# Batched matmul of transposed inputs: b loaded for two batches at once, eight rows per partition, one transpose for both

## The chip, the cores and the metric

One core of a Trainium2 chip. The metric is the device time of one execution in microseconds (us); lower is better. Engines are named as the profile names them: PE is TensorE's matmul, PEld its weight load, DVE is VectorE, ACT is ScalarE, SP is SyncE, whose queue (SPq) issues every DMA here. "16 engines" are the core's DMA engines.

## The reference

```python
batch, m, k, n = 16, 512, 512, 512
a: (batch, k, m) float32,  b: (batch, n, k) float32

def reference(a, b):
    return np.matmul(a.transpose(0, 2, 1), b.transpose(0, 2, 1)).astype(np.float32)
```

Per batch 1 MB of a and 1 MB of b come in and 1 MB of result goes out: 50.33 MB in all. b has its contraction axis k last, so it must be transposed on the chip.

## The kernel before

Each batch is one round of a loop: load b and a, cast a to bf16 on ACT, transpose b on PE in f32 into PSUM, cast the transposed b to bf16 on DVE (the "cast" of this document), multiply, evict the result on ACT and DVE in turn, store the result of six batches earlier.

```python
a_v = a.rearrange("b (ki ko) m -> b ki ko m", ko=KO)      # 4 consecutive rows (8 KB) per partition
b_v = b.rearrange("b (no ni) k -> b ni no k", ni=P)       # rows 128 apart: pieces of 2 KB
out_v = out.rearrange("b (mi mo) n -> b mi mo n", mo=MO)  # 8 KB per partition
# ... pools: a 3, b 3, a in bf16 4, bt 3, o 8 buffers; psum_t 4, psum_o 4 banks
LAG = 6
for i in range(B):
    b_sb = b_pool.tile([P, NO, K], f32)
    nc.sync.dma_start(b_sb, b_v[i])
    # ... load a, cast it to a_bf on ACT
    for rk in range(KO):
        bt_ps = psum_t.tile([P, N], f32)
        for no in range(NO):
            nc.tensor.transpose(bt_ps[:, no * P:(no + 1) * P], b_sr[:, no, rk, :], identity)
        nc.vector.tensor_copy(bt_sb[:, rk, :], bt_ps)     # the cast: contiguous in, contiguous out
    # ... 16 matmuls into o_ps, evictions to o_sb by ACT and DVE in turn
    if i >= LAG:
        emit_out_dma(i - LAG)
```

## Time and profile before

| | before |
|---|---|
| time, median of the first 3 runs | 129.39 us (129.38 to 129.58) |
| span in the profile | 127.8 us |
| DMA queue, share of 16 engines' span | 97.5% |
| one cast of transposed b (DVE) | 683 ns |

From the page of the kernel before: the busy line, then rows of the view that cuts the span into 40 equal slices. A digit is the busy share of that slice in tenths; PEclk is the clock granted to TensorE; DMA is the mean of the 16 engines.

```profile
PE 92.5 (72%) x504; PEld 60.6 (47%) x512; DVE 61.5 (48%) x96; ACT 54.8 (43%) x97; POOL 0.7 (1%) x6
...
PE   0099999999999995768767796877779777670000
DVE  0053668586774865463544727355472635640000
PEclk9999999999999999999999999999999999998555
DMA  3999999999999999999999999999999999999980
...
q1 hardware_dynamic: 13056, 50.33, 97.5%
```

The DMA row is 9 nearly from end to end while PE and DVE have room: the kernel is bound by its transfers. The groups of instructions say what one instruction costs; the columns are busy us, mean ns of one, then the idle time just before them and who ended it.

```profile
L80 PE MATMUL o_ps<-bt_sb,a_bf 128*128 128x512 bf16 x248 | 59.0, 385 | 9.1 <-ACT a_bf L60 8.7
...
L73 DVE CAST bt_sb<-bt_ps 128x512 bf16<-128x512 f32 x64 | 40.0, 683 | 14.7 <-PE bt_ps L68 14.7
L68 PE MATMUL bt_ps<-identity,b_sb 128*128 128x128 f32 x256 | 35.7, 295 | 12.8 <-DMA b_sb<-in_b_dram 12.8
```

### The profile page before, as it was taken

What the parts mean: (1) busy time and instruction counts of PE and PEld (TensorE: products, weight loads), DVE (VectorE), ACT (ScalarE), POOL (GpSimd) and SP (SyncE); (2) the same over time, 40 slices, a digit from 0 to 9 for tenths busy, and PEclk for the clock granted to TensorE, in tenths of its full rate; (3) what the DMA queues carried; (4) which work ended last, traced back from release to release, by engine and by line L of the source; (5) the groups of instructions that cost most, each with busy time, mean ns of one, the idle gap of its engine ahead of it and who ended that gap; (6) DMA issues with size and microseconds to landing.
All of it is one profiled execution on the core that took longest, in us unless ns stands there. A gap on an engine that the chain in (4) does not pass through costs nothing.

```text
span 127.8 us, 1405 instructions
## 1 busy us (share of the span) xinstructions
PE 92.5 (72%) x504; PEld 60.6 (47%) x512; DVE 61.5 (48%) x96; ACT 54.8 (43%) x97; POOL 0.7 (1%) x6
## 2 busy tenths in 40 slices
PE   0099999999999995768767796877779777670000
PEld 0094858678586763364634536353364634430000
DVE  0053668586774865463544727355472635640000
ACT  4026747646674635407163460816337072540000
POOL 2000000000000000000000000000000000000000
PEclk9999999999999999999999999999999999998555
DMA  3999999999999999999999999999999999999980
GB/s 90 402 370 422 406 399 420 382 409 398 404 417 415 417 419 394 416 410 429 420 410 423 406 436 405 416 426 413 427 402 431 412 424 418 426 428 428 426 346 36
DMA packets 13063, 50.42 MB, mean 394 GB/s; under 512 B 768, under 2 KB 768, under 8 KB 8960
## 3 DMA queue, kind: packets, MB, share of 16 engines
q1 hardware_dynamic: 13056, 50.33, 97.5%
q8 instruction: 4, 0.07, 0.2%
q14 instruction: 3, 0.02, 0.0%
HBM read 33.55 MB, written 16.78 MB: 394 GB/s over the span
## 4 chain that ended last, share of the span: by engine, by line
DMA 50%; PE 34%; SPq 3%; ACT 1%; issue 1%; DVE 1%; ACTq 0%
DMA a_sb<-in_a_dram 32%; PE o_ps L80 22%; DMA out_dram<-o_sb 13%; PE bt_ps L68 12%; DMA b_sb<-in_b_dram 4%; SPq L56 3%; ACT a_bf L60 1%; DVE o_sb L90 1%; ACT o_sb L88 0%; ACTq L60 0%; SPq L50 0%
## 5 line engine op out<-in xcount | busy, mean ns | idle before, releaser
L80 PE MATMUL o_ps<-bt_sb,a_bf 128*128 128x512 bf16 x248 | 59.0, 385 | 9.1 <-ACT a_bf L60 8.7
L60 ACT CAST a_bf<-a_sb 128x512 bf16<-128x512 f32 x64 | 34.9, 615 | 39.6 <-DMA a_sb<-in_a_dram 39.5
L73 DVE CAST bt_sb<-bt_ps 128x512 bf16<-128x512 f32 x64 | 40.0, 683 | 14.7 <-PE bt_ps L68 14.7
L68 PE MATMUL bt_ps<-identity,b_sb 128*128 128x128 f32 x256 | 35.7, 295 | 12.8 <-DMA b_sb<-in_b_dram 12.8
L80 PEld LDWEIGHTS <-a_bf 128*128 128x128 bf16 x256 | 27.3, 115 | 35.8 <-ACT a_bf L60 17.7
L68 PEld LDWEIGHTS bt_ps<-identity,b_sb 128*128 128x128 f32 x256 | 33.9, 211 | 17.5 <-PE o_ps L80 8.5
L90 DVE COPY o_sb<-o_ps 128x512 f32<-128x512 f32 x32 | 22.1, 692 | 38.9 <-PE o_ps L80 21.9
L88 ACT COPY o_sb<-o_ps 128x512 f32<-128x512 f32 x32 | 18.8, 586 | 19.0 <-PE o_ps L80 18.9
L60 ACT ACT_TABLE_LOAD x1 | 1.3, 1283 | 0.7 <-PEq L111 0.7
masks.py:199 POOL TENSOR_SCALAR_AFFINE_SELECT identity<-identity 128x128 f32<-128x128 f32 x1 | 0.3, 292 | 0.1
masks.py:197 POOL MEMSET identity<- 128x128 f32 x1 | 0.2, 204 | 0.3 <-POOLq L111 0.3
L111 POOL MEMSET const-bfloat16-1.0<- 128x1 bf16 x1 | 0.1, 101 | 0.0
L111 POOL MEMSET const-uint8-127<- 128x1 uint8 x1 | 0.1, 101 | 0.0
L111 POOL MEMSET const-float32-0.0<- 128x1 f32 x1 | 0.1, 98 | 0.2 <-issue 0.2
L111 POOL MEMSET const-float32-1.0<- 128x1 f32 x1 | 0.1, 98 | 0.0
## 6 DMA issues: line engine op xcount, KB each, us to landing
b_sb<-in_b_dram SPq DMA_DIRECT2D x16, 1024.0 KB, 15.4
a_sb<-in_a_dram SPq DMA_DIRECT2D x16, 1024.0 KB, 17.3
out_dram<-o_sb SPq DMA_DIRECT2D x16, 1024.0 KB, 17.4
```

The costliest lines, as they stand in the source:

```text
L56: nc.sync.dma_start(a_sb, a_v[i])
L60: nc.scalar.copy(a_bf[:, rk, :], a_sb[:, rk, :])
L68: nc.tensor.transpose(bt_ps[:, no * P:(no + 1) * P], b_sr[:, no, rk, :], identity,)
L73: nc.vector.tensor_copy(bt_sb[:, rk, :], bt_ps)
L80: nc.tensor.matmul(o_ps, a_br[:, rk, rm, :], bt_sb[:, rk, :], start=(rk == 0), stop=(rk == KO - 1),)
L88: nc.scalar.copy(o_sb[:, rm, :], o_ps)
L90: nc.vector.tensor_copy(o_sb[:, rm, :], o_ps)
L111: nc = _bacc.Bacc("TRN2", target_bir_lowering=False, num_devices=1)
```

## The change

The intent: b arrives in pieces of 2 KB, the other two tensors in pieces of 8 KB. If each partition takes eight consecutive rows of b, its piece is 16 KB. 64 partitions then hold one batch of 512 rows, so one load of 2 MB covers two batches, and each 128x128 transpose covers both. A transposed block holds every eighth row of each batch, so the cast has to put its columns back in order: it writes bf16 elements eight apart. The stores follow three batches behind rather than six, with buffers moved between pools.

```diff
-    b_v = b.rearrange("b (no ni) k -> b ni no k", ni=P)
+    b_v = b.rearrange("(h g) (ni r) k -> h (g ni) r k", g=G, r=R)      # G = 2, NI = 64, R = 8
...
-    a_pool bufs=3, ac_pool bufs=4, bt_pool bufs=3, o_pool bufs=8; LAG = 6
+    a_pool bufs=5, ac_pool bufs=3, bt_pool bufs=2, o_pool bufs=6; LAG = 3
...
+        if i % G == 0:
+            b_sr = b_sb.rearrange("p r (pk rk) -> p r rk pk", rk=KO)
+            bt_pair = bt_pool.tile([P, G, KO, N], cdt)
+            bt_w = bt_pair.rearrange("p g rk (ni r) -> p rk r g ni", r=R)
+            H = R // 2
+            for rk in range(KO):
+                for h in range(2):
+                    bt_ps = psum_t.tile([P, H, G, NI], f32)
+                    for r in range(H):
+                        nc.tensor.transpose(bt_ps[:, r, :, :], b_sr[:, h * H + r, rk, :], identity)
+                    nc.vector.tensor_copy(bt_w[:, rk, h * H:(h + 1) * H, :, :], bt_ps)
+        bt_sb = bt_pair[:, i % G, :, :]
```

(The pool lines are abridged.) In the cast, the last `tensor_copy`, the innermost loop of the output is `ni`, and neighbouring `ni` lie eight bf16 elements, 16 bytes, apart.

## The prediction

> **What bounds it now.** The DMA engines, not TensorE. In the 40-slice view the mean busy share of the 16 DMA engines is 9 tenths or more from the second slice to the last but two, while PE falls to 6-8 tenths in mid-run. The queue view gives the one hardware queue 97.5% of 16 engines' span (127.8 us, so 124.6 us); about 3.2 us of the span is not DMA. The waits view agrees: ScalarE waits 39.5 us for loads of a, PE's transposes 12.8 us for b.
>
> **What the packets cost.** In the trace's packet records, b moves as 8192 packets of 2 KB, 84 ns each (median; mean 86.2); a and out as 4096 packets of 8 KB, 309 ns (mean 312.6). So b takes 8192 x 86.2 / 16 = 44.1 us, a and out 80.0 us, 768 semaphore packets 0.4 us. The two medians fit 9 ns fixed plus 27.3 bytes/ns. The Trainium skill, "DMA: Bandwidth & Descriptors", section "Why small descriptors are slow", says a fixed overhead is paid for each packet (about 3 cycles); this trace agrees in kind, with 9 ns fitted for it.
>
> **The change.** b's rows are now eight consecutive per partition: 16 KB in one piece on both sides, 8 transfers of 2 MB rather than 16 of 1 MB. If one packet carries 16 KB, the fit gives about 609 ns, about 616 with the mean's inflation: 1024 x 616 / 16 = 39.4 us for b (an estimate; two 8 KB packets would give 40.0). Saved: 4.1 to 4.7 us of DMA time, all on the critical resource.
>
> Compute does not change in count: 256 f32 transposes, 64 eviction casts (683 ns), 256 matmuls, the same ScalarE casts. DVE's casts now write bf16 with a stride of 16 bytes. The Trainium skill, "SBUF — State Buffer", note on cachelines, puts the free stride for bf16 at about 8 elements, exactly this one; no run shows it yet. I expect 680-750 ns. PE per pair (about 3.9 us transposes, 7.4 us matmuls) stays under the pair's roughly 14.8 us of DMA.
>
> **Where the change could cost.** Start: the first transposes need 2 MB of b (about 7.3 us rather than 6.2) and there are 32 of them before the first matmul, so the first store is issued at about 18-19 us instead of behind six batches. By then 8 MB of loads are queued, enough until about 21.5 us: I expect no DMA gap. Steady state: the stores three behind leave several loads queued. End: after the last load of a lands, three stores (7.5 us) cover the last batch's cast, matmuls and evictions (5 us, and 1.1 us to first byte): at most about 1 us of gap. The smaller lag alone is worth nothing.
>
> **Predicted time: 124.7 us** (129.39 minus 4.7), 80% range 123.4 to 127.0. Faster by over 2%: 0.88; within 2%: 0.11; slower by over 2%: 0.01.
>
> **What would show each step.** Right: no 2 KB packets left, queue share near 97% of a span of about 123 us, 16 KB packets near 610 ns, DVE casts below 750 ns, DMA slices all 9 from the second to the last two or three. Wrong: b's packets costing more than 26 bytes/ns allows; a slice at 20-25 us or near 112-118 us below 9, i.e. DMA waiting for the first or the last stores.
>
> **What would make it wrong.** Strided DVE writes at 1.2 us or more, which would delay the first store past the prefetched loads; stores and loads disturbing each other more at the HBM; uneven DMA engines making the last one late; packets still being cut at 2 KB.

## More of the kernel before

The timeline of DVE alone in one batch (start, duration, instruction, count):

```profile
85.69 2.48 DVE L73 CAST bt_sb<-bt_ps 128x512 bf16<-128x512 f32 x4 [0.80 <-PE bt_ps L68]
90.28 0.69 DVE L90 COPY o_sb<-o_ps 128x512 f32<-128x512 f32 x1 [2.11 <-ACT a_bf L60]
91.73 0.69 DVE L90 COPY o_sb<-o_ps 128x512 f32<-128x512 f32 x1 [0.76 <-PE o_ps L80]
```

Four casts take 2.5 us of a batch's 7.6 us or so; then DVE waits for data.

## The result

The changed kernel is correct and takes **226.16 us** (median of 6 runs, 223.12 to 233.59) against 129.38 us (129.17 to 129.58) for the kernel before: 1.74 times as long. Ratios in this document are the mean time of one kernel's fast runs over that of the other's fast runs of the same rounds, so not quite the ratio of the quoted medians; here 1.742, 95% interval 1.733 to 1.752. Two of the six runs, among them the profiled one, fell in the slow state, in which the same kernel takes some per cent longer at a lower granted TensorE clock (here 233.5 us, clock 0.673; the four fast runs had 0.713 to 0.779). So the profile shown here is that of a later, unchanged repetition of the changed kernel in the fast state (226.23 us in the profiled run; median 226.11 us).

The same parts of its page:

```profile
PE 132.0 (59%) x504; PEld 71.5 (32%) x512; DVE 168.7 (75%) x96; ACT 53.5 (24%) x97; POOL 0.7 (0%) x6
...
PE   0457398465974469445792549545693548934590
DVE  0299926998289973999459993999549994599931
PEclk9995559655595559955599569955599555995697
DMA  7999009990399605995089913996069930630044
...
q1 hardware_dynamic: 5760, 50.33, 58.2%
...
L80 DVE CAST bt_pair<-bt_ps 128x512 bf16<-128x512 f32 x64 | 147.2, 2624 | 9.9 <-PE bt_ps L77 9.9
L88 PE MATMUL o_ps<-bt_pair,a_bf 128*128 128x512 bf16 x248 | 84.1, 500 | 36.8 <-DVE bt_pair L80 34.4
L77 PE MATMUL bt_ps<-identity,b_sb 128*128 128x128 f32 x256 | 49.4, 343 | 49.9 <-DVE bt_pair L80 41.2
```

The kernel is no longer bound by DMA: the DMA row falls to 0 again and again and the queue's share is 58%. DVE is busy 168.7 us instead of 61.5, and all of the increase is in one group: 64 casts as before, with as many elements each, at 2624 ns instead of 683. (The records of successive casts overlap a little, so eight of them take 18.4 us, 2.3 us each.) Transposes and matmuls now both wait mostly for these casts (41.2 of their 49.9 us and 34.4 of 36.8 us of waiting), where they waited for loads and for a's cast before.

DVE's timeline of one pair of batches:

```profile
89.63 18.39 DVE L80 CAST bt_pair<-bt_ps 128x512 bf16<-128x512 f32 x8
109.18 0.69 DVE L98 COPY o_sb<-o_ps 128x512 f32<-128x512 f32 x1 [1.16 <-issue]
111.69 0.69 DVE L98 COPY o_sb<-o_ps 128x512 f32<-128x512 f32 x1 [1.81 <-PE o_ps L88]
114.08 0.69 DVE L98 COPY o_sb<-o_ps 128x512 f32<-128x512 f32 x1 [1.70 <-PE o_ps L88]
115.53 0.69 DVE L98 COPY o_sb<-o_ps 128x512 f32<-128x512 f32 x1 [0.76 <-PE o_ps L88]
116.14 18.41 DVE L80 CAST bt_pair<-bt_ps 128x512 bf16<-128x512 f32 x8
```

A pair takes 116.14 - 89.63 = 26.5 us: 18.4 us of casts, then 8.1 us in which PE finishes the matmuls of both batches and makes the first transposes of the next pair. The two blocks stand one after the other, because PE runs the next pair's transposes only after this pair's matmuls (in its timeline the last of these run from 108.08 us, and the next transposes start at 115.33). This was one pair; over the run they differ. The first cast starts at 9.85 us and the eighth pair's first cast at 194.33 us, so seven pairs take 26.4 us each on the mean. The last pair is done at 219.4 us, and the last store brings the span to 224.2 us.

The loads themselves did what was hoped. In the packet records b moves as 1024 packets of 16 KB, 611 ns each (median).

### The profile page after: what moved, and what is told of

Read it like the earlier page. It is cut to its first block, busy times and chain, and to the rows that moved or that the text cites. A ratio compares the mean times of both kernels' runs of the same rounds, so it can differ in the third digit from the quotient of the medians.

```text
span 231.5 us, 1368 instructions
## 1 busy us (share of the span) xinstructions
PE 139.4 (60%) x504; PEld 73.7 (32%) x512; DVE 168.7 (73%) x96; ACT 53.4 (23%) x97; POOL 0.7 (0%) x6
## 3 DMA queue, kind: packets, MB, share of 16 engines
q1 hardware_dynamic: 5760, 50.33, 56.3%
## 5 line engine op out<-in xcount | busy, mean ns | idle before, releaser
L80 DVE CAST bt_pair<-bt_ps 128x512 bf16<-128x512 f32 x64 | 147.2, 2618 | 9.7 <-PE bt_ps L77 9.7
L88 PE MATMUL o_ps<-bt_pair,a_bf 128*128 128x512 bf16 x248 | 90.4, 533 | 38.0 <-DVE bt_pair L80 36.2
L77 PE MATMUL bt_ps<-identity,b_sb 128*128 128x128 f32 x256 | 50.5, 348 | 48.7 <-DVE bt_pair L80 40.1
L88 PEld LDWEIGHTS <-a_bf 128*128 128x128 bf16 x256 | 34.3, 134 | 93.2 <-issue 80.5
L77 PEld LDWEIGHTS bt_ps<-identity,b_sb 128*128 128x128 f32 x256 | 39.5, 213 | 58.7 <-DVE bt_pair L80 49.3
L96 ACT COPY o_sb<-o_ps 128x512 f32<-128x512 f32 x32 | 18.7, 586 | 162.5 <-PE o_ps L88 162.5
```

The lines of the kernel that those rows point to most:

```text
L77: nc.tensor.transpose(bt_ps[:, r, :, :], b_sr[:, h * H + r, rk, :], identity)
L80: nc.vector.tensor_copy(bt_w[:, rk, h * H:(h + 1) * H, :, :], bt_ps)
L88: nc.tensor.matmul(o_ps, a_br[:, rk, rm, :], bt_sb[:, rk, :], start=(rk == 0), stop=(rk == KO - 1),)
L96: nc.scalar.copy(o_sb[:, rm, :], o_ps)
```

## The experiments

The theory after this reading: **a bf16 write with 16 bytes between consecutive elements is slow by itself, and it stands in series with the matmuls.** Rivals: the store lag of three or the shared block of 32 transposes; the four-level loop shape of the cast; loads writing to SBUF at the same time; the slow state.

### The disputed cost alone

The kernel of this run makes copies of 512 elements per partition, five of each kind in a row, with no load and no TensorE work beside them. Its output is wrong, which doesn't matter for the time.

```diff
+    for _ in range(5): nc.vector.tensor_copy(st(wb, 8), ps1)   # st(t, s): 512 elements of t, s apart
+    ... the same for other strides, f32, the change's own pattern, other orders, ScalarE
```

> Copies of 128x512 alone, five of each kind in a row, with no DMA and no TensorE running (the result is wrong on purpose). Theory (the bf16 write at a stride of 16 bytes is slow by itself): bf16 from PSUM at strides 1, 2 and 4 elements about 0.68 us, at 8 elements (16 bytes) and 16 elements about 2.3 to 2.6 us; the change's own pattern about 2.6 us; the same addresses written four neighbours at a time about 0.7 us; a contiguous write with the same loop shape 0.68 us. Rival A (the four-level loop shape is slow): stride 8 in one plain loop is 0.68 us, and the contiguous write with the same loop shape is 2.6 us. Rival B (the engine waits for SBUF because loads write it at the same time): all kinds are about 0.68 us here. Rival C (any 2-byte write that is not packed is slow): stride 2 is already 2.3 us or more, and f32 at the same strides is not slow.

Ten of the groups of its profile. L54, L57, L60, L63 and L66 write bf16 at strides of 1, 2, 4, 8 and 16 elements; L75 writes f32 at 4 elements; L81 is the change's own pattern; L84 writes the same addresses as L81, four neighbours at a time; L90 is a contiguous write with as many loop levels as the change's pattern; L105 is ScalarE at a stride of 8.

```profile
L105 ACT CAST wa<-ps 128x512 bf16<-128x512 f32 x5 | 12.1, 2425 | 0.2
L81 DVE CAST wf<-ps 128x512 bf16<-128x512 f32 x5 | 12.1, 2421 | 0.2
L63 DVE CAST wf<-ps 128x512 bf16<-128x512 f32 x5 | 12.1, 2420 | 0.2
L66 DVE CAST wf<-ps 128x512 bf16<-128x512 f32 x5 | 11.5, 2293 | 0.2
...
L60 DVE CAST wf<-ps 128x512 bf16<-128x512 f32 x5 | 6.5, 1290 | 0.2
...
L75 DVE COPY wf<-ps 128x512 f32<-128x512 f32 x5 | 5.3, 1054 | 0.2
L57 DVE CAST wf<-ps 128x512 bf16<-128x512 f32 x5 | 3.6, 722 | 0.1
...
L84 DVE CAST wf<-ps 128x512 bf16<-128x512 f32 x5 | 3.5, 691 | 0.2
...
L90 DVE CAST wf<-ps 128x512 bf16<-128x512 f32 x5 | 3.5, 691 | 0.2
L54 DVE CAST wf<-ps 128x512 bf16<-128x512 f32 x5 | 3.4, 678 | 0.0
```

The stride alone, in one plain loop and on an idle chip, costs 2420 ns against 678. The loop shape is innocent: the change's pattern costs the same 2421, and a contiguous write with that loop shape took 691. So is traffic of loads to SBUF: there was none. (ScalarE's copies ran beside L81 to L90, but not beside L63, which took the same time as L81.) The rival "any unpacked 2-byte write" fails at a stride of 2 (722). One point was not as expected: a stride of 4 bf16 elements is already dear (1290 ns). And the order decides, not the addresses: L84 fills the same places as L81 in 691 ns. It reads PSUM at a stride of 512 bytes to do so, and that reading costs nothing visible.

### The change with its cast in long runs

```diff
-nc.vector.tensor_copy(bt_w[:, rk, h * H:(h + 1) * H, :, :], bt_ps)
+nc.vector.tensor_copy(
+    bt_pair[:, :, rk, h * 256:(h + 1) * 256].rearrange("p g (r ni) -> p g r ni", r=H),
+    bt_ps.rearrange("p r g ni -> p g r ni"))
```

> The changed kernel with its casts writing runs of 256 bf16 instead of single elements 16 bytes apart; the columns of the result come out in another order, so it is wrong on purpose. Theory (the strided write is the whole loss, and the prediction's DMA part holds): casts 0.68 us, time 124.7 us (123.5 to 127), queue share of 16 engines near 97%. Rivals (the store lag of 3, or both batches' transposes in one block, leave the DMA idle): casts 0.68 us but the time stays over 135 us with DMA gaps.

126.81 us (125.78 to 127.58), ratio to before 0.980 (0.975 to 0.986); casts 685 ns. Everything else of the change was left in place. The 99 us are gone when only the cast's write is changed.

### The change with the same addresses, in runs of four

```diff
-nc.vector.tensor_copy(bt_w[:, rk, h * H:(h + 1) * H, :, :], bt_ps)
+nc.vector.tensor_copy(
+    bt_pair[:, :, rk, :].rearrange("p g (ni r) -> p g ni r", r=R)[:, :, :, h * H:(h + 1) * H],
+    bt_ps.rearrange("p r g ni -> p g ni r"))
```

> The changed kernel with the same bf16 addresses written, but each cast writes the four neighbouring rows of a group one after the other (runs of 8 bytes) and reads PSUM at a stride instead; the result stays right. Theory (the cost is a step of 16 bytes or more between consecutive writes): every fourth write still steps, so casts about 0.7 to 1.1 us and a time of 124.7 to 128 us. If the cost belongs to the addresses and not to their order: 2.6 us and about 226 us. If strided PSUM reads cost as much: over 2 us too.

Correct, 126.81 us (126.09 to 127.31), ratio 0.982 (0.979 to 0.985). From its page, the DMA row and the cast:

```profile
DMA  5999999999999999999999999999999999999973
...
L80 DVE CAST bt_pair<-bt_ps 128x512 bf16<-128x512 f32 x64 | 40.2, 684 | 24.0 <-PE bt_ps L77 23.8
```

The order of the same writes is worth 99 us. The prediction's model of the rest holds too: no DMA gap near the first store (the first one was issued at 19.1 us). But 124.7 us was not reached.

### The change with stores six behind

```diff
-    LAG = 3        (o_pool bufs=6)
+    LAG = 6        (o_pool bufs=8)
```

> The changed kernel with stores six batches behind and eight output buffers, as before. Theory (DVE's strided casts bound it): no help, 220 to 230 us, DVE cast still about 2.6 us. Rival (loads stuck in the queue behind stores that wait): clearly under 200 us, because the sync engine issues loads earlier.

225.08 us (224.26 to 225.97), ratio 1.741; casts 2624 ns. In the changed kernel SP waits 170 us for result tiles, which looks like a queue blocked by early stores. It is a symptom: letting the stores wait longer changes nothing.

### Stores six behind, with the cast repaired

```diff
 (the kernel with runs of four)
-    LAG = 3        (o_pool bufs=6)
+    LAG = 6        (o_pool bufs=8)
```

> The kernel with runs of four (126.8 us with stores three behind) with stores six behind and eight output buffers. Theory (the 2 us that it lacked of the predicted 124.7 us are DMA gaps around the last stores, which wait for the last batches' compute): 124.5 to 125.5 us, DMA slices 9 until the last two, and less spread. Rival (16 KB packets cost more than estimated, or the later start of compute does): no change, 126.5 to 127 us.

126.53 us (126.33 to 126.80), ratio 0.978 (0.975 to 0.981), beside 126.81 and 0.982 (0.979 to 0.985) at three: no clear difference. The expectation failed, and the rival's figure (126.5 to 127) came true; the 2 us missing to 124.7 are not the last stores' wait. They are found below.

### The kernel before with only longer pieces of b

```diff
-    b_v = b.rearrange("b (no ni) k -> b ni no k", ni=P)
+    b_v = b.rearrange("b (ni no) k -> b ni no k", no=NO)          # 4 consecutive rows, 8 KB
...
-            nc.vector.tensor_copy(bt_sb[:, rk, :], bt_ps)
+            nc.vector.tensor_copy(
+                bt_sb[:, rk, :].rearrange("p (ni no) -> p ni no", no=NO),
+                bt_ps.rearrange("p (no ni) -> p ni no", no=NO))
```

> The kernel before with one thing changed: four consecutive rows of b in each partition, so one 8 KB piece per partition and batch, with the order put back by a strided PSUM read and a contiguous bf16 write. No pairs, store lag 6. Theory (the packet size is worth it, and PSUM reads at a stride are free): b in 8 KB packets of about 310 ns, 40 us of 16 engines rather than 44, casts 0.69 us, 125.0 us (124.5 to 126). Rival (reading PSUM at a stride of 512 bytes, or pairs, matter): no faster than 128.5 us.

Correct, **126.42 us** (126.31 to 126.57), ratio 0.977 (0.974 to 0.979): no slower than the best of the repaired pair kernels (0.978), with two statements changed and no pairs. The order is put back while reading PSUM, the write is contiguous, and the cast takes 683 ns as before. Going from 8 KB to 16 KB shows no gain. The rival (128.5 us or more) failed, but the expected 125.0 us (124.5 to 126) was missed too.

The profile also shows why 124.7 us and 125.0 us were too low. These lines are of a view that gives busy times in a stretch of the run (20 to 100 us); the last three numbers are granted clock, DMA share and GB/s. First the kernel before:

```profile
20.00:100.00 80.00, 67.20 (x376) 43.71 (x380) 46.30 (x73) 39.52 (x72) 0.00 (x0) 1.00 1.03 414
```

The kernel with single batches and 8 KB pieces:

```profile
20.00:100.00 80.00, 69.19 (x395) 45.43 (x393) 47.95 (x77) 39.35 (x72) 0.00 (x0) 1.00 1.01 423
```

The kernel with pairs, 16 KB pieces and runs of four:

```profile
20.00:100.00 80.00, 67.61 (x370) 46.18 (x374) 45.76 (x71) 36.59 (x68) 0.00 (x0) 0.96 1.01 425
```

The DMA share of the kernel before is 1.03: the records of its packets overlap, so their sum, on which the prediction built, counts more time than passed. The trace tells which: in half-microsecond pieces of this stretch the share is 1.05 where 2 KB packets fill at least 90% of the packet time, and 1.00 where they fill under 10%. What counts is the rate: 50.33 MB at 414 GB/s are 121.6 us, at 423 GB/s 119.0 us, so 2.6 us are to be had; 129.28 - 126.42 = 2.9 us were.

### The kernel before with only the strided write

```diff
-            nc.vector.tensor_copy(bt_sb[:, rk, :], bt_ps)
+            nc.vector.tensor_copy(
+                bt_sb[:, rk, :].rearrange("p (ni r) -> p r ni", r=8),
+                bt_ps.rearrange("p (r ni) -> p r ni", r=8))
```

> The kernel before with only the cast's write order changed to single bf16 elements 16 bytes apart (columns of the result permuted: wrong on purpose). Theory (this write alone, in series with the matmuls, makes the loss): casts 2.3 to 2.6 us; per batch about 9.1 us of casts, then most of the matmuls, at a clock that drops while TensorE waits: 13.5 to 16 us, 215 to 255 us in all. Rival (it needs the pairs, their shared block of 32 transposes, or two buffers): under 160 us, as DVE's own work is only 10.5 us per batch against 7.6 us of DMA.

233.84 us (232.35 to 234.63), ratio 1.805; casts 2594 ns. No pairs, no shared transposes, lag six: that one write is enough to make the loss. The group of the casts, then two batches' casts in DVE's timeline:

```profile
L73 DVE CAST bt_sb<-bt_ps 128x512 bf16<-128x512 f32 x64 | 148.4, 2594 | 7.5 <-PE bt_ps L68 7.4
...
105.09 9.26 DVE L73 CAST bt_sb<-bt_ps 128x512 bf16<-128x512 f32 x4
...
118.77 9.26 DVE L73 CAST bt_sb<-bt_ps 128x512 bf16<-128x512 f32 x4
```

Four casts take 9.26 us and the next four start 13.7 us after the first, so 4.4 us of a batch lie outside the casts.

### The same at half the stride

As above with `r=4`: single elements 8 bytes apart.

> The kernel before with its casts writing single bf16 elements 8 bytes apart (1.29 us each alone on the chip; result permuted, wrong on purpose). Theory (the four casts of a batch stand in series with its matmuls): in the run with 16 bytes a batch took 13.7 us, 9.3 of casts and 4.4 of the rest; with about 5.1 us of casts it should take 9.0 to 9.6 us, 145 to 160 us in all. Rival (only a DVE that is busier than the DMA counts): DVE's work is 6.5 us per batch, under the 7.6 us of DMA, so 129 to 131 us.

134.92 us (134.84 to 135.04), ratio 1.042 (1.040 to 1.044); casts 1329 ns. Neither number came true. The series is there: four casts in 4.75 us, a batch every 7.55 us. But the part outside the casts is 2.8 us and not 4.4, because TensorE now keeps its clock (0.996, against 0.775 in the profile of the stride of 16 bytes): the nine matmuls after a batch's last cast take 2.10 us here and 3.72 there. So a batch takes just about what its transfers take (121.6 us over 16 batches are 7.6 us), and only the end of the run is lost:

```profile
DMA  3999999999999999999999999999999999996315
...
L73 DVE CAST bt_sb<-bt_ps 128x512 bf16<-128x512 f32 x64 | 76.0, 1329 | 7.3 <-PE bt_ps L68 7.3
```

A cast twice as long costs 5 us here; nearly four times as long, 105 us. In these two runs the large loss comes where casts and matmuls in series outlast the transfers.

### TensorE kept busy while it waits

Nine transposes of the identity after each four real ones, and twelve before each of the first four matmuls of a pair; nothing reads them. PSUM room for them came from one of the four result banks.

```diff
+    warm = psum_w.tile([P, P], f32)                      # psum_o bufs 4 -> 3
...
+                    for _ in range(9): nc.tensor.transpose(warm, identity, identity)
...
+                if i % G == 0 and rm == 0:
+                    for _ in range(12): nc.tensor.transpose(warm, identity, identity)
```

> The changed kernel, with its strided casts, and transposes of the identity added on TensorE in every stretch in which it waits for a cast; nothing reads them. Theory (part of the loss is TensorE's clock, which falls while it waits for DVE, so the matmuls after the casts take 0.42 us from one to the next rather than 0.22): granted clock over 0.9 rather than 0.67 to 0.78, matmuls near 380 ns, and 190 to 210 us although TensorE has more to do. Rival (the casts are all of it): no gain, 223 us or more.

222.86 us (222.77 to 223.02), ratio 1.722. The clock did what was expected, the time did not:

```profile
PEclk9999999999999999999999999999999999999999
...
L85 DVE CAST bt_pair<-bt_ps 128x512 bf16<-128x512 f32 x64 | 149.6, 2682 | 9.5 <-PE bt_ps L80 9.5
```

A pair still takes 25.8 us, of which 18.7 are casts. The expectation forgot that the clock can only shorten the remaining 8.1 us, and it shortened them to 7.1. That is a lower bound for the clock's part, as the added work and the missing bank pushed all but three of the pair's matmuls behind the last cast. The fast profile of the changed kernel holds a cleaner comparison. In its pair that starts at 116.14 us TensorE was granted the full clock (1.00) after the casts, and the rest of the pair took 6.6 us; in the pair before, at 0.74, it took the 8.1 us. If all pairs were as short as this one (25.0 us instead of the mean 26.4), the run would be some 11 us shorter, an estimate: a small part of the 97 us lost. The granted clock of the changed kernel's fast runs goes with their times (223.57 us at 0.772, 226.46 us at 0.713), while the casts did not move: 18.4 us a pair in the slow profile as well as in the fast one. With TensorE idle for 1 to 3 us at a time, the PEclk row of the changed kernel alternates between 5 and 9. The Trainium skill, "TensorE: Matmul & The Clock Gate", "Part 1: The HAM clock gate", describes a clock of this kind: half rate is the default, and activity lifts it. This agrees in kind, with 5 tenths as the lowest value of the row; how long TensorE must wait for the clock to fall was not measured.

### Half of the strided casts on ScalarE

```diff
-                    nc.vector.tensor_copy(bt_w[...], bt_ps)
+                    if h == 0: nc.vector.tensor_copy(dst, bt_ps)
+                    else:      nc.scalar.copy(dst, bt_ps)
```

> The changed kernel with every second strided cast given to ScalarE, which writes at this stride as slowly (2.4 us). Theory (the pair's casts are a serial block of 18.4 us before its matmuls): the block shrinks to about 10 to 14 us (four strided casts on ScalarE with one or two batches' casts of a, 0.55 us each, between them), a pair takes 18 to 22 us instead of 26 to 27, and the time is 155 to 185 us; still far over 129. Rival (SBUF cannot take such writes any faster whatever engine makes them): casts slow each other to about 4 to 5 us and the time stays above 215 us.

Correct, 166.63 us (164.87 to 167.44), ratio 1.282.

```profile
L84 ACT CAST bt_pair<-bt_ps 128x512 bf16<-128x512 f32 x32 | 75.8, 2622 | 17.5 <-PE bt_ps L77 17.5
L82 DVE CAST bt_pair<-bt_ps 128x512 bf16<-128x512 f32 x32 | 74.9, 2616 | 9.8 <-PE bt_ps L77 9.8
```

Casts take 2616 ns on DVE and 2622 on ACT, at the same time: the two engines do not slow each other. In the pair that starts at 85.78 us the block of casts ends after 11.7 us, and the next pair's casts start after 18.55 us, both as expected. Shortening the block of casts shortens the run, by 59 us, which is what a block in series must do.

### More copies alone

> Copies of 512 elements per partition alone (wrong on purpose). Theory S (each step to a new 16-byte unit costs, and neighbours in it are free): runs of two bf16 at 8-byte steps about 0.7 us, runs of two at 16-byte steps about 1.05 to 1.3 us (256 steps), runs of four at 16 bytes 0.69 us, runs of four at 32 bytes 0.69 us, single elements at 6 and 12 bytes about 1.0 and 1.9 us. Theory P (SBUF writes of less than 4 bytes are what is slow): runs of two (4 bytes) at 16-byte steps 0.7 us. Fewer partitions (64, 32): unchanged at about 2.4 us if the cost is in each lane; half and a quarter if lanes share something. From SBUF instead of PSUM: f32 at 16 bytes about 0.6 us, bf16 at 16 bytes 1.3 us as measured before, whatever the source type.

Both microbenchmarks together, mean ns of one copy of 512 elements per partition:

| written, source PSUM in f32 | bytes from one write to the next | ns |
|---|---|---|
| single bf16 | 2, 4, 6, 8, 12, 16, 32 | 678, 722, 1007, 1290, 1854, 2420, 2293 |
| single f32 | 4, 8, 16, 32 | 691, 691, 1054, 1072 |
| runs of two bf16 | 8, 16 | 683, 691 |
| runs of four bf16 | 16, 32 | 691, 691 |
| single bf16 on ScalarE | 2, 8, 16 | 586, 1291, 2425 |
| single bf16, source SBUF in f32 | 2, 8, 16 | 427, 735, 1300 |
| single bf16, source SBUF in bf16 | 2, 16 | 294, 1299 |
| single f32, source SBUF in f32 | 4, 16 | 427, 620 |

Two of its groups: the stride of 16 bytes on 32 partitions (L84), and runs of two at 16-byte steps (L60).

```profile
L84 DVE CAST wf<-ps 32x512 bf16<-32x512 f32 x5 | 12.0, 2406 | 0.2
...
L60 DVE CAST wf<-ps 128x512 bf16<-128x512 f32 x5 | 3.5, 691 | 0.1
```

The cost does not depend on the number of partitions, so the partitions do not share it. Theory S fell: runs of two at 16-byte steps are free. Theory P fits that, but does not say why a single bf16 every 4 bytes is nearly free (722 ns), why a single f32, a whole 4-byte word, costs 1054 ns at 16 bytes, nor why the source matters. Between 6 and 16 bytes (and 722 ns at 4 bytes lies on it too) a single bf16 grows along a straight line, (2420 - 1007) / 10 / 512 = 0.28 ns for each byte of stride. The mechanism stays open; the numbers are enough for use.

### The changed kernel again

> The changed kernel once more, unchanged, for a profile in the fast state to set beside the slow one: 223 to 226.5 us, granted clock 0.70 to 0.79, casts 2.6 us as before, a pair every 26 to 26.6 us, of which about 18.4 us are its eight casts in a row. If the state, not the casts, made the loss, casts or pair time would differ by more than the 1 us between the states.

226.11 us (223.57 to 226.46), ratio 1.741; clock 0.71 to 0.77. The pair of 26.5 us with 18.4 us of casts, shown above, is its profile. In the slow profile a pair (the one from 117.48 us) took 27.3 us with the same 18.4 us. The state is not the cause.

## Why the prediction was wrong

**The step that failed:** "DVE's casts now write bf16 with a stride of 16 bytes [...] I expect 680-750 ns." They took 2624 ns in the kernel (2.3 us each in a row) and 2420 ns alone. The prediction took one figure from the Trainium skill, "SBUF — State Buffer", the note on cachelines: strides are free up to 8 bf16 elements. The same note says that at least two accesses must fall in one 16-byte line. At a stride of 16 bytes every access falls in a new one, so the note's own reason spoke against its figure; and even two per line (8 bytes) took 1290 ns here. The warning was in the prediction's last paragraph, but only as a delay of the first store.

**What followed from it.** Even as a sum the mis-sized term would have moved the bound: 8 x 2.3 us of casts and 4 x 0.69 us of evictions are 21 us of DVE per pair, above the predicted 14.8 us of DMA. The prediction set only PE's own work of a pair (3.9 + 7.4 us) against the pair's DMA time. In fact casts and matmuls stand in series, 18.4 + 8.1 us. The split over two engines and the strided write put alone into the kernel before both confirm that.

**What held.** DMA bounds the kernel before, and the changed one once its cast is repaired: its 126.81 us then lie in the predicted range of 123.4 to 127.0. 16 KB packets took 611 ns at the median (predicted 609). With the cast repaired, the first store came at 19.1 us without a DMA gap, and the smaller lag alone is worth nothing (225.08 against 226 us; 126.53 against 126.81).

**What was off in size.** The DMA gain was put at 4.7 us by summing packet records. With the order put back in the PSUM read 2.5 to 2.9 us came. The records of the 2 KB packets overlap (share 1.03), so their sum was too large, and the mean of the 16 KB packets, which the sum uses, was 630 ns in the kernel with runs of four, not 616. The measured rates in mid-run, 414 and 423 to 425 GB/s, give the right size.

**What stays open.** Why narrow writes at a stride cost what they do. TensorE's clock is 1.5 of the 8.1 us beside the casts, by one pair against the next in one profile; no run held all else equal.

## What to carry to other kernels

When a better DMA layout leaves elements out of order, put the order back while reading PSUM and write SBUF in runs: runs of four bf16 or more cost nothing here, single bf16 elements 16 bytes apart took 3.6 times as long on VectorE and 4.1 times on ScalarE. Measure such an access pattern alone, before building on a rule about strides, above all when the pattern lies exactly at the rule's limit. And when durations add up to more than the time in which they ran, size a gain by rates, not by the sum.

## What the Trainium skill lacked or had wrong

- "SBUF — State Buffer", note on cachelines: it gives 4 f32 and 8 bf16 elements as free strides. Measured writes from PSUM: f32 691 ns at strides of 1 and 2, 1054 at 4; bf16 678 at 1, 722 at 2, 1290 at 4, 2420 at 8. Its other condition, two accesses in a 16-byte line, fits runs of two bf16 at 16-byte steps, which are free (691), but not single bf16 elements 8 bytes apart, also two in a line (1290). It does not say that the cost stays the same with fewer partitions (2406 on 32).
- "VectorE: DVE Perf Modes", "Mode 1× (REGULAR) — the baseline": one result per cycle, and odd strides are said to work, with no cost named. Reading PSUM at a stride had almost none (691 ns at 512 bytes, against 678); writing SBUF at one had (2420).
- "ScalarE: Activation LUTs" has no figure for strided writes: 586 ns contiguous, 1291 at 8 bytes, 2425 at 16.
- "DMA: Bandwidth & Descriptors", "Why small descriptors are slow": its worked example is a descriptor of 256 bytes. 2 KB against 8 KB pieces for a third of the bytes is still 414 against 423 GB/s; 16 KB adds almost nothing (425).
- "Memory Cachelines" in "Advanced Engine Details and Errata" asks for contiguous pairs in PSUM, for matmuls; that DVE reads PSUM at a stride of 512 bytes at almost no cost (691 ns) stands on no page that was read.
